# Six edits to a bidirectional gated encoder layer on one core: an 18th pair, sums on VectorE, loads and small steps reordered

## The chip, the core and the metric

The kernel runs on one core of a Trainium2 chip. The metric is device microseconds of one execution, as the median of several runs. The engines are TensorE (PE, with PEld for its weight loads), VectorE (DVE), ScalarE (ACT), GpSimd (POOL) and SyncE (SP, which here only issues DMAs). Times in the text are microseconds (us) unless marked ns.

## The reference, cut to what matters

One layer over x of 1024 positions and 1024 channels, in float32:

```
h  = RMSNorm(x)
glu_in, q, v, z_f, z_b, og, g_a, g_b = split(h @ W_in)        # 1024 + 7*1024 columns
a  = silu(LayerNorm(dwconv31(glu(glu_in)))) @ pw_w            # 512 channels -> 1024
f  = lb + (1 - lb) * sigmoid(z);  key = (1 - lb) * sigmoid(-z) # lb from a softmax of two logits
o  = scan_fwd(silu(q), key_f, v, log f_f) + scan_bwd(...)     # 8 heads of 128, gated linear recurrence
b  = (headnorm(o) * silu(og)) @ o_w
x  = x + (sigmoid(g_a) * a + sigmoid(g_b) * b) @ w_out
h2 = RMSNorm(x)
x  = x + (silu(dwconv3(h2 @ W_gate)) * (h2 @ W_up)) @ w_down  # 2816 hidden
y  = RMSNorm(x)
```

## The kernel before, in words

All activations are kept transposed, channels on partitions and 512 positions ("half" 0 or 1) in a page of 128x512. For precision each fp32 operand is split into a high and a low part, so that every product of 128x128 by 128x512 is three matmuls, in `mm3` (L144 to L146): high by high, high by low, low by high. A split is a cast on ACT (L122) and a subtraction on DVE (L119).

Work is handed out as *jobs*. A job has a `prep` (load of its weights and their split) and a `run`, a generator that gives back control after every piece of 6 matmuls. `run_jobs` runs jobs in order and prepares one job ahead; with `lead` 4 it does so after the first four pieces of the job that runs. `Stream.fill(n)` runs n pieces; this is how matmuls are put between the steps of other work. The order on TensorE is the order in which the program emits it; on the other engines and their DMA queues a planner orders the instructions.

Two kinds of jobs matter here:

- `std_job`: 128 output columns, both halves, 8 blocks of rows: 16 pieces, 96 matmuls.
- `pair_job`: two such column blocks together by Strassen's scheme in the form of seven products of half size, 14 pieces, 84 matmuls. The seven products run in the order 1, 2, 6, 7, 5, 4, 3 (`run`). Their weights are combinations of the four quarters: products 1 and 2 use the rows as loaded; 7 and 5 use `col`, to which a DMA with accumulation added the other column block; 6 and 3 use the rows after two more accumulating DMAs, issued by POOL (L242: `wr<-sw`, `wr<-wr`), which overwrite the rows and so come after the first split has read them. Weight pages "wp" are a ring of four.

The stages, with their times in the profile of before:

1. 0 to 77: load x (`load_x`, four tiles of SP loads), transposes of x for the residual (`residual`, which writes d_x0), first norm of half 0 (`first_norm`), the GLU's first jobs between. `load_vectors` loads a group of small vectors as rows, `turn_vectors` transposes them on TensorE and copies them (L349). v_n holds the first norm's weights.
2. To 471: the rest of the GLU, then the combinations for the pairs (`h_combos`, pages in the ring "su" of four), the lower bounds `lbw` (L691 on), and the stream `s_pairs` of the `NPAIRS` pairs of input columns; between its pieces DVE does the 31 taps of the convolution (`conv_steps`, L755), and then come the LayerNorm and the start of the pointwise jobs. In the LayerNorm of each half, `total` adds the four channel pages into one, and a matmul with ones (L424 for the sum of squares) adds over partitions.
3. To 518.9: the pointwise jobs (8 for each half, two pieces each, operands `ch` in the pool gp0). They are put into the jobs' queue at its front as each half's operands are done:

```
        for i in range(ND):
            job = std_job(
...
            pw_jobs.append(job)
            jobs.insert(at + i, job)
    s_pairs.drain()
```

4. To 975: the scan. Pools p1 and gp0 are released and `hp` takes their place. What input columns the pairs left over (`rest = todo[2 * NPAIRS :]`) become standard jobs of the stream `dense`, with which the scan's steps are interleaved:

```
    cur = Base(scan_inputs(0))
    ins = scan_inputs(1)
    dense.fill(21)
```

`scan_inputs` loads q (L858) and z (L861) of a head and half and makes f and the keys; `scan_base` makes products over blocks of eight positions on DVE (L840, L843: DE, qF, kG); `scan_levels` then doubles the block, each level with a copy on ACT (L945) and matmuls (L948), and between the levels `dense.fill(1.3)`. The pieces left over run at the end of the scan.
5. To 1158: output projection of the scan, merge with the gates, `w_out`, x2 and the FFN's operands.
6. To 1600.8: 22 pairs `ffn_job` (gate and value columns of a block of 128 hidden channels). The second norm's factor `rstd2` is made by two matmuls with ones (L424, then L416) while the first pieces of `s_ffn` run. The evacuation `evac(0, half, ...)` of a gate multiplies by `rstd2` (L1282); after half 1 come the three taps (ACT L1288, DVE L1292, in pages c of the ring "tm" of four), silu, the second factor (L1301), the product with the value (L1302) and the store to d_g.
7. To the end: the down projection in five groups of 4, 4, 5, 5 and 4 blocks of hidden channels; `load_g` loads the g pages of a group (pages of the ring "ev" of three) and splits them; `first_evac` (L1364) copies the first group's sums to `xr`, which later groups add to; the last group adds x2 and makes the last norm.

Of the kernel before, what the change touches and what calls it, by code (L numbers as in the profile page):

```python
# [14 lines left out]
AF = mybir.ActivationFunctionType  # L15
ALU = mybir.AluOpType
# [2 lines left out]
P = 128  # L19
FILL = 1.3  # L20
CONV_FILL = 1.6
NPAIRS = 17
LN_FILL = 6
LN_LAST = 14
GLU_FIRST = 4
# [4 lines left out]
H = 512  # L30
# [15 lines left out]
def tile_hybrid_encoder(  # L46
# [24 lines left out]
    V, A, G, T = nc.vector, nc.scalar, nc.gpsimd, nc.tensor  # L71
# [9 lines left out]
    NH = D // DK  # L81
# [10 lines left out]
    def nm(s):  # L92
        uid[0] += 1
        return f"{s}_{uid[0]}"
# [3 lines left out]
    def bank(tag):  # L98
        return ps.tile([P, H], F32, tag=tag, name=nm(tag), bufs=BANKS[tag])

    def page(pool, tag, bufs, dt=F32):
        return pool.tile([P, H], dt, tag=tag, name=nm(tag), bufs=bufs)
# [4 lines left out]
    def ev():  # L107
        return page(mp, "ev", 3)

    def hx():  # L110
        return page(mp, "hx", 32, F32R)
# [209 lines left out]
    def load_x(half):  # L321
        for i in range(half * 4, half * 4 + 4):
            xt = p0.tile([P, D], F32, tag="xt", name=nm("xt"), bufs=S // P)
            nc.sync.dma_start(xt, x[0, i * P : (i + 1) * P, :])
            x_in.append(xt)

    load_x(0)

    vec_off = {}
    rows_in = []  # L330

    def load_vectors(name, parts):
        n = sum(k for _, _, k in parts)
        r = mp.tile([P, P], F32, tag="tm", name=nm("vr"), bufs=4)
        o = 0
        for key, ap, k in parts:
            nc.sync.dma_start(r[o : o + k, :], ap)
            vec_off[key] = (name, o)
            o += k
        v = cp.tile([P, n], F32, name=name)  # L340
        rows_in.append((v, r, n))
        return v

    def turn_vectors(tag="ob"):
        b = bank(tag)
        for i, (v, r, n) in enumerate(rows_in):
            T.transpose(b[:, i * P : i * P + n], r[:n, :], ident[:n, :n])
        for i, (v, r, n) in enumerate(rows_in):
            V.tensor_copy(v, b[:, i * P : i * P + n])  # L349
        rows_in.clear()  # L350

    def rview(ap):
        r = ap[0]
        if len(r.shape) == 2:
            r = r.rearrange("a b -> (a b)")
        return r.rearrange("(r c) -> r c", c=P)

    vecs = {"v_n": load_vectors("v_n", [("attn", rview(attn_norm_w), ND)])}
    others = {
        "v_a": [  # L360
            ("ffn", rview(ffn_norm_w), ND),
# [71 lines left out]
    def first_norm():  # L433


        xs = x_in[:4]
        ss = cp.tile([P, 4], F32, name=nm("ss"), tag="ss", bufs=2)
        rs = cp.tile([P, 4], F32, name=nm("rs4"), tag="rs4", bufs=1)
        xn = []
        for i, xt in enumerate(xs):  # L440
            t = p0.tile([P, D], F32, tag="xn", name=nm("xn"), bufs=4)
            A.activation(t, xt, AF.Square, accum_out=ss[:, i : i + 1])
            rstd_small(rs[:, i : i + 1], ss[:, i : i + 1], D)
            V.tensor_scalar(t, xt, rs[:, i : i + 1], None, op0=ALU.mult)
            xn.append(t)

        def residual(i, g, tag):
            b = bank(tag)
            for k in range(4):
                T.transpose(  # L450
                    b[:, k * P : (k + 1) * P], xs[i][:, (4 * g + k) * P : (4 * g + k + 1) * P], ident
                )
            t = page(p0, "xr", 7)
            V.tensor_copy(t, b)
            nc.sync.dma_start(
                d_x0[:, i, 4 * g : 4 * g + 4, :], t.rearrange("p (k t) -> p k t", k=4)
            )

        def turn(b, i, k):
            T.transpose(b[:, i * P : (i + 1) * P], xn[i][:, k * P : (k + 1) * P], ident)  # L460

        residual(0, 0, "mm")
        residual(0, 1, "mm")
        turn_vectors("mm")
        banks = [bank(t) for t in ("sc", "tr", "sc", "tr", "ob")]
        for i in range(4):
            for k, b in enumerate(banks):
                turn(b, i, k)
        yield
        late = {2: (1, 0, "mm"), 3: (1, 1, "tr"), 4: (2, 0, "ob")}  # L470
        late |= {5: (2, 1, "sc"), 6: (3, 0, "tr"), 7: (3, 1, "sc")}
        for k in range(ND):
            b, g = banks[k], vec("attn", k)
            hi, lo, raw = hx(), hx(), page(p0, "raw", ND)
            A.activation(hi, b, AF.Copy, scale=g)
            V.scalar_tensor_tensor(lo, b, g, hi.bitcast(F32), op0=ALU.mult, op1=ALU.subtract)  # L476
            A.activation(raw, b, AF.Copy, scale=g)
            nc.sync.dma_start(d_h[k][0], raw)
            ht[1 if k < NK2 else 2].append((hi, lo))
            yield  # L480
            if k + 5 < ND:
                b = bank(("sc", "tr", "sc")[k])
                for i in range(4):
                    turn(b, i, k + 5)
                banks.append(b)
            if k in late:
                residual(*late[k])
# [43 lines left out]
    for j in range(NCW):  # L531
        g = gp0.tile([P, PAD + S + PAD], F32, tag="gl", name=nm("gl"), bufs=NCW)
# [144 lines left out]
    p1 = tc.alloc_tile_pool(name="p1", bufs=1, reuse_waits="tile")  # L677
# [13 lines left out]

    lbl = vecs["v_a"][:, vec_off["lb"][1] : vec_off["lb"][1] + 2 * NH]
    lbw = cp.tile([P, 4, 2 * NH], F32, name="lbw")
    V.tensor_tensor(lbw[:, 0, :], lbl, lbl, op=ALU.max)
    V.tensor_tensor(lbw[:, 0, :], lbl, lbw[:, 0, :], op=ALU.subtract)
    A.activation(lbw[:, 1, :], lbw[:, 0, :], AF.Exp)
    V.reciprocal(lbw[:, 2, :], lbw[:, 1, :])
    V.tensor_tensor(lbw[:, 1, :], lbw[:, 1, :], lbw[:, 2, :], op=ALU.mult)
    V.tensor_tensor(lbw[:, 2, :], lbw[:, 1, :], lbw[:, 1, :], op=ALU.subtract)
# [39 lines left out]

    jobs = collections.deque(in_pair(n) for n in range(1, NPAIRS))  # L740
    jobs.appendleft((lambda: w_pair0, pair0[1]))
# [22 lines left out]


    def total(ts, o):
        G.tensor_tensor(o, ts[0], ts[1], op=ALU.add)
        for t in ts[2:]:
            G.tensor_tensor(o, o, t, op=ALU.add)
        return o  # L770

    pw_jobs = []
# [42 lines left out]

    rest = todo[2 * NPAIRS :]
    rest_jobs = [std_job(in_cols(c), ND, h_std, e) for c, e in rest[:-2]]
# [4 lines left out]
    for k in range(NK2):  # L822
        t = load(d_h[k][1])
        h12.append(split(hx(), hx(), t, V))
    dense = Stream(run_jobs(rest_jobs))
# [297 lines left out]
    NI = 2 * NH  # L1123
    cur = Base(scan_inputs(0))
    ins = scan_inputs(1)
    dense.fill(21)
    pending = Stream(iter(()))
    for h in range(NH):
        Tt = hp.tile([P, 2, 2, 4], F32, tag="Tt", name=nm("Tt"), bufs=3)
# [139 lines left out]
    def ffn_job(j):  # L1269
        g = gp[j % 2]  # L1270
        val = [None, None]

        def evac(e, half, x0, x1=None, op=None):
            if e == 1:
                val[half] = page(fu, "ft", 4)
                V.tensor_tensor(val[half], x0, x1, op=op)
                return
            gh = g[:, 1 + half * H : 1 + (half + 1) * H]
            if x1 is not None:
                V.tensor_tensor(gh, x0, x1, op=op)  # L1280
                x0 = gh
            V.tensor_tensor(gh, x0, rstd2[half], op=ALU.mult)  # L1282
            if half == 0:
                return
            for hf in range(2):
                o = hf * H
                c = tmp()
                A.activation(  # L1288
                    c, g[:, o : o + H], AF.Identity, scale=vec("fdw", j), bias=vec("fdb", j)
                )  # L1290
                for k in (1, 2):
                    V.scalar_tensor_tensor(  # L1292
                        c,
                        g[:, o + k : o + k + H],
                        vec("fdw", k * NF + j),
                        c,
                        op0=ALU.mult,
                        op1=ALU.add,
                    )
                A.activation(c, c, AF.Silu)  # L1300
                V.tensor_tensor(c, c, rstd2[hf], op=ALU.mult)  # L1301
                V.tensor_tensor(val[hf], val[hf], c, op=ALU.mult)  # L1302
                nc.sync.dma_start(d_g[j][hf], val[hf])

        return pair_job(
            w_cols(ffn_w_up, 0, ND, j * P),
            w_cols(ffn_w_up, 0, ND, DFF + j * P),
            NK2,
            lambda i: h2[i],
            fw,  # L1310
            fu,
            evac,
            su=3,
        )

    s_ffn = Stream(run_jobs([ffn_job(j) for j in range(NF)], 4))
    s_ffn.fill(2)
    stats = [rstd_over_partitions(sq, D, "sc", sq) for sq in sq_sum]
    for st in stats:
        next(st)  # L1320
    s_ffn.fill(2)
    rstd2 = [next(st) for st in stats]

    def late_parts(i, src):
# [24 lines left out]
        return hx() if next(n_g) == 0 else page(fd, "gx", 16, F32R)  # L1349

    groups = [4, 4, 5, 5, 4]
    gs, jobs = [], []

    def load_g(f0, n):
        for f in range(f0, f0 + n):
            gs.append([])
            for half in range(2):
                t = ev()
                nc.sync.dma_start(t, d_g[f][half])
                gs[-1].append(split(g_page(), g_page(), t, V))  # L1360

# [132 lines left out]
```

## Time and profile before

| what | us |
|---|---|
| median of 3 runs | 1859.93 (1857.55 to 1863.16) |
| profiled execution | 1873.26 |
| span of the profile (first to last instruction) | 1871.5 |
| PE busy | 1788.6 (96%) |
| DVE busy | 1275.7 (68%) |
| ACT busy | 796.2 (43%) |
| POOL busy | 185.8 (10%) |
| mean granted clock of TensorE | 0.984 |

The profiled execution was 0.7% longer than the median of the runs. The busy time of PE counts a matmul until its modelled end, and matmuls overlap; so the time of a stretch of matmuls is read from its length and the number of matmuls in it. The view of windows gives both, with the granted clock of the stretch. Waits of an engine are read from the view of waits (engine, tile and line that waited, what released it; then the sum in us, how often, the longest) or from the brackets at the end of a row of the timeline.

### The profile page before, as it was taken

How to read it: one execution, taken by the hardware profiler on the slowest of the kernel's cores; microseconds unless marked ns; L12 is line 12 of the kernel's file. 1: busy time of each engine (PE TensorE's matmuls, PEld its weight loads, DVE VectorE, ACT ScalarE, POOL GpSimd, SP SyncE). 2: the span in 40 equal slices, each digit the busy share in tenths (PEclk: the TensorE clock that was granted, in tenths of full speed). 3: DMA queues.
4: the chain of work that ended last, by engine and by line, in shares of the span. 5: the costliest groups of instructions: out<-in, count | busy, mean ns of one | idle time of the engine just before them, and what ended most of it. 6: DMA issues, size and time to landing. Idle time of an engine off the chain costs nothing.

```text
span 1871.5 us, 23768 instructions
## 1 busy us (share of the span) xinstructions
PE 1788.6 (96%) x8574; PEld 1481.4 (79%) x8574; DVE 1275.7 (68%) x1874; ACT 796.2 (43%) x1483; POOL 185.8 (10%) x197
## 2 busy tenths in 40 slices
PE   7989999999999999999989999899999999899996
PEld 6868777777778888888878787688888888788885
DVE  4599999534479999999835565666666667534445
ACT  6443333234545566556442244443444434522124
POOL 1201111213000000000000001111111111000000
PEclk9999999999999999999999999999999999999998
DMA  7658878775653333332238665676776765633134
GB/s 268 213 141 185 184 170 198 184 170 130 208 186 96 113 113 117 98 108 91 74 110 239 191 193 190 152 156 144 150 153 149 156 146 130 208 97 95 55 86 169
DMA packets 323468, 281.42 MB, mean 150 GB/s; under 512 B 14734, under 2 KB 246934, under 8 KB 323350
## 3 DMA queue, kind: packets, MB, share of 16 engines
q1 hardware_dynamic: 272886, 240.05, 41.4%
q0 software_dynamic: 50464, 39.85, 14.9%
q8 instruction: 67, 1.10, 0.3%
q14 instruction: 51, 0.42, 0.1%
HBM read 188.09 MB, written 71.83 MB: 139 GB/s over the span
## 4 chain that ended last, share of the span: by engine, by line
PE 45%; DVE 23%; DMA 18%; ACT 6%; issue 5%; POOL 1%; SPq 0%; ACTq 0%; POOLq 0%; DVEq 0%
PE mm L144 12%; PE mm L145 12%; PE mm L146 12%; DMA wr<-wr 4%; DVE wp L119 3%; DMA wr<-sw 3%; DMA sw<-in_w_in_dram 3%; DMA tm<-d_a 3%; DVE kG L840 2%; DVE acc L755 2%; PE sc L144 2%; PE sc L146 2%; PE sc L145 2%; DVE qF L840 2%; DVE DE L840 2%
## 5 line engine op out<-in xcount | busy, mean ns | idle before, releaser
L144 PE MATMUL mm<-hx,wp 128*128 128x512 f32 x1176 | 480.1, 408 | 23.8 <-DVE ev L541 6.8
L146 PE MATMUL mm<-hx,wp 128*128 128x512 f32 x1176 | 464.9, 395 | 1.9 <-DVE wp L119 1.9
L145 PE MATMUL mm<-hx,wp 128*128 128x512 f32 x1176 | 464.6, 395 | 0.5 <-DVE hx L476 0.5
L122 ACT CAST wp<-wr 128x1024 fp32r<-128x1024 f32 (+2 forms) x193 | 176.7, 915 | 344.8 <-PE mm L145 188.3
L119 DVE TENSOR_TENSOR wp<-wr,wp 128x1024 fp32r<-128x1024 f32 (+2 forms) x193 | 203.4, 1054 | 123.0 <-ACT wp L122 116.2
L144 PEld LDWEIGHTS mm<-hx,wp 128*128 128x128 f32 x1176 | 224.7, 191 | 72.9 <-DVE ev L541 9.7
L146 PEld LDWEIGHTS mm<-hx,wp 128*128 128x128 f32 x1176 | 224.1, 191 | 52.5 <-DVE wp L119 3.7
L145 PEld LDWEIGHTS mm<-hx,wp 128*128 128x128 f32 x1176 | 224.7, 191 | 43.0 <-DVE hx L476 0.8
L755 DVE SCALAR_TENSOR_TENSOR acc<-gl,v_b,acc 128x1024 f32<-128x1024 f32 x120 | 150.0, 1284 | 0.5
L1370 DVE TENSOR_TENSOR xr<-mm,xr 128x512 f32<-128x512 f32 x48 | 33.1, 690 | 80.4 <-PE mm L146 80.4
L948 PE MATMUL sc<-qF,A 128*128 128x128 f32 x512 | 69.8, 280 | 13.3 <-DVE qF L840 13.1
L948 PEld LDWEIGHTS sc<-qF,A 128*128 128x128 f32 x512 | 65.2, 195 | 20.4 <-issue 14.9
L242 POOL DMA_DIRECT2D wr<-sw x38 | 33.8, 889 | 442.8 <-DVE wp L119 153.1
L122 ACT CAST wq<-sw 128x1024 fp32r<-128x1024 f32 x39 | 41.0, 1051 | 77.1 <-PE mm L145 59.5
L945 ACT COPY A<-kG 128x512 f32<-128x512 f32 x64 | 39.6, 618 | 73.8 <-DVE kG L840 51.3
L1292 DVE SCALAR_TENSOR_TENSOR tm<-gp,v_a,tm 128x512 f32<-128x512 f32 x88 | 65.6, 746 | 3.3 <-ACT tm L1288 2.5
L144 PE MATMUL mm<-hy,wp 128*128 128x512 f32 x156 | 62.2, 399 | 3.1 <-ACT su L270 2.9
L145 PE MATMUL mm<-hy,wp 128*128 128x512 f32 x156 | 61.9, 396 | 0.7 <-DVE hy L119 0.7
L270 ACT COPY su<-mm 128x512 f32<-128x512 f32 x78 | 45.1, 578 | 39.2 <-PE mm L146 39.2
L144 PE MATMUL tr<-hx,wp 128*128 128x512 f32 x156 | 61.4, 394 | 0.0
L146 PE MATMUL mm<-hy,wp 128*128 128x512 f32 x156 | 61.1, 392 | 0.0
L144 PE MATMUL sc<-hy,wq 128*128 128x512 f32 x156 | 61.1, 392 | 0.0
(322 smaller groups left out, 3601.5 us busy)
## 6 DMA issues: line engine op xcount, KB each, us to landing
wr<-in_w_in_dram SPq DMA_DIRECT2D x53, 512.0 KB
sw<-in_ffn_w_up_dram SPq DMA_DIRECT2D x44, 256.0 KB
sw<-in_ffn_w_up_dram POOLq DMA_DIRECT2D x22, 512.0 KB, 9.2
wr<-in_ffn_w_up_dram SPq DMA_DIRECT2D x22, 512.0 KB
d_g<-ft SPq DMA_DIRECT2D x44, 256.0 KB
ev<-d_g SPq DMA_DIRECT2D x44, 256.0 KB
wr<-sw POOLq DMA_DIRECT2D x38, 256.0 KB, 3.2
wr<-wr POOLq DMA_DIRECT2D x38, 256.0 KB, 4.8
```

Source lines behind the costliest of these rows:

```text
L119: eng.tensor_tensor(lo, src, hi.bitcast(F32), op=ALU.subtract)
L122: A.copy(hi, src)
L144: T.matmul(acc, whi[:, k, :], ahi, start=first, stop=False, skip_group_check=again)
L145: T.matmul(acc, whi[:, k, :], alo, start=False, stop=False, skip_group_check=again)
L146: T.matmul(acc, wlo[:, k, :], ahi, start=False, stop=last, skip_group_check=again)
L242: G.dma_start(o, a, accum_op=ALU.add)
L270: A.copy(t, acc)
L755: V.scalar_tensor_tensor(acc, g[:, k : k + S], tap(k), acc, op0=ALU.mult, op1=ALU.add)
L840: V.tensor_tensor(o, a, b, op=op)
L945: A.copy(A_t.rearrange("p (b x e) -> p b x e", x=2, e=h), pairs(kG, h))
L948: T.matmul(b[:, c * P : (c + 1) * P].rearrange("p (b x e) -> p b x e", x=2, e=h), A_t[:, c * P : (c + 1) * P], view(qF, c * P, [[2 * h, P ...
L1292: V.scalar_tensor_tensor(c, g[:, o + k : o + k + H], vec("fdw", k * NF + j), c, op0=ALU.mult, op1=ALU.add,)
```

## The change

Six edits:

- The first norm's weights are loaded ahead of x, and their transposes run ahead of the two residual ones.
- The lower bounds' first two steps work in a page of the ring "su" instead of the constant tile `lbw`, so that they wait for their turn in that ring.
- `total` adds on VectorE instead of GpSimd.
- There are 18 pairs instead of 17, so that two column blocks fewer are left for `dense`, and `dense.fill(21)` ahead of the scan is `dense.fill(5)`.
- The FFN multiplies half 0 of the gate by `rstd2` only when half 1 comes, and 5 pieces instead of 2 run between the two matmuls of the second norm's sums.
- The g loads take their pages from the rings "ev" and "tm" in a cycle of seven.

```diff
-NPAIRS = 17
+NPAIRS = 18
...
-    load_x(0)
-
     vec_off = {}
...
     vecs = {"v_n": load_vectors("v_n", [("attn", rview(attn_norm_w), ND)])}
+    load_x(0)
...
+        turn_vectors("mm")
         residual(0, 0, "mm")
         residual(0, 1, "mm")
-        turn_vectors("mm")
         banks = [bank(t) for t in ("sc", "tr", "sc", "tr", "ob")]
...
     lbw = cp.tile([P, 4, 2 * NH], F32, name="lbw")
-    V.tensor_tensor(lbw[:, 0, :], lbl, lbl, op=ALU.max)
-    V.tensor_tensor(lbw[:, 0, :], lbl, lbw[:, 0, :], op=ALU.subtract)
-    A.activation(lbw[:, 1, :], lbw[:, 0, :], AF.Exp)
+    lbt = page(p1, "su", 4)[:, : 2 * NH]
+    V.tensor_tensor(lbt, lbl, lbl, op=ALU.max)
+    V.tensor_tensor(lbt, lbl, lbt, op=ALU.subtract)
+    A.activation(lbw[:, 1, :], lbt, AF.Exp)
...
     def total(ts, o):
-        G.tensor_tensor(o, ts[0], ts[1], op=ALU.add)
+        V.tensor_tensor(o, ts[0], ts[1], op=ALU.add)
         for t in ts[2:]:
-            G.tensor_tensor(o, o, t, op=ALU.add)
+            V.tensor_tensor(o, o, t, op=ALU.add)
         return o
...
-    dense.fill(21)
+    dense.fill(5)
...
             gh = g[:, 1 + half * H : 1 + (half + 1) * H]
-            if x1 is not None:
+            if half == 0:
                 V.tensor_tensor(gh, x0, x1, op=op)
-                x0 = gh
-            V.tensor_tensor(gh, x0, rstd2[half], op=ALU.mult)
-            if half == 0:
                 return
+            V.tensor_tensor(g[:, 1 : 1 + H], g[:, 1 : 1 + H], rstd2[0], op=ALU.mult)
+            V.tensor_tensor(gh, x0, rstd2[1], op=ALU.mult)
             for hf in range(2):
...
-    s_ffn.fill(2)
+    s_ffn.fill(5)
     rstd2 = [next(st) for st in stats]
...
-    gs, jobs = [], []
+    gs = []
+    n_in = itertools.cycle([ev, tmp, ev, tmp, ev, tmp, tmp])
...
-                t = ev()
+                t = next(n_in)()
                 nc.sync.dma_start(t, d_g[f][half])
```

## The prediction

> **What bounds the kernel now.** I read the page first (sections 1 and 2), then the work of each stage in windows, then the waits and the timelines around the places that the change touches.
>
> ```profile
> span 1871.5 us, 23768 instructions
> PE 1788.6 (96%) x8574; PEld 1481.4 (79%) x8574; DVE 1275.7 (68%) x1874; ACT 796.2 (43%) x1483; POOL 185.8 (10%) x197
> DVE  4599999534479999999835565666666667534445
> ```
> ```profile
> 0.00:77.00 77.00, 67.59 (x320) 55.51 (x321) 32.70 (x43) 43.73 (x69) 16.98 (x34) 0.98 0.76 255
> 77.00:340.00 263.00, 251.23 (x1081) 203.88 (x1080) 250.48 (x275) 101.81 (x143) 38.44 (x36) 0.99 0.74 174
> 494.60:518.90 24.30, 24.06 (x103) 18.85 (x103) 9.17 (x13) 11.84 (x21) 0.63 (x2) 1.00 0.69 212
> 518.90:547.40 28.50, 28.50 (x127) 23.61 (x126) 18.88 (x29) 18.65 (x29) 0.53 (x1) 1.00 0.73 226
> 547.40:975.00 427.60, 402.58 (x2538) 353.65 (x2537) 372.72 (x691) 226.51 (x528) 15.62 (x16) 0.99 0.31 99
> 1202.00:1600.80 398.80, 397.96 (x1730) 324.12 (x1729) 263.67 (x352) 165.14 (x232) 64.36 (x59) 1.00 0.69 149
> ```
>
> In a window row the second number is its length, then busy time of PE, weight loads, DVE, ACT, POOL, then the granted clock. TensorE is the bound nearly everywhere: 96% of the span, 397.96 of 398.80 us in the FFN. DVE is full as well in two stages, the first pairs with the convolution's taps (250.48 of 263) and the scan (372.72 of 427.60, nines and eights in its slices). So removed matmuls pay where PE is alone, and a wait of PE costs unless other matmuls stand in front of it. From 518.9 to 547.4, 126 products of 128x512 run without a gap: 28.50/126 = 0.226 us each, the price of one below.
>
> **Part 1, the 18th pair and the fill of 21 that becomes 5.** A pair takes 84 products where two plain jobs took 96. Pairs and the pointwise jobs share one queue, in which pair 17 comes to stand between the two pointwise halves: the jobs of the first half were put in ahead of it, those of the second half behind it, since the queue has not reached it by then. What follows the second half is the scan, and it starts like this:
>
> ```profile
> 518.61 0.40 PE L146 MATMUL mm<-ch,wp 128*128 128x512 f32 x1
> 519.04 0.46 SPq L858 DMA_DIRECT2D q<-d_q  x1
>   POOL DE L834: 42.6, 1
> 521.67 0.92 SPq L861 DMA_DIRECT2D zi<-d_z  x2
> 525.69 0.63 ACT L862 ACTIVATE k<-zi 128x512 f32<-128x512 f32 x1 [3.11 <-DMA zi<-d_z]
> 535.03 1.22 DVE L119 TENSOR_TENSOR wp<-wr,wp 128x1024 fp32r<-128x1024 f32 x1
> 542.34 1.22 DVE L840 TENSOR_TENSOR kG<-Kh,DE 128x1024 f32<-128x1024 f32 x1
> 545.55 0.61 ACT L945 COPY A<-kG 128x512 f32<-128x512 f32 x1
> 547.43 1.05 PE L948 MATMUL sc<-qF,A 128*128 128x128 f32 x8
> ```
>
> The first row is the last pointwise matmul. The scan's pages lie where the pointwise operands lay: POOL's first memset of DE waited 42.6 us for these matmuls, and the scan's q load goes out 0.4 us after the last of them starts. Then a chain runs: z loads, sigmoids, the base on DVE, a copy, and the first matmul of the scan at 547.43, 28.6 us after the last pointwise product (its successor started at 518.85). In the kernel before, the 21 dense pieces of 6 products (126 x 0.226 = 28.5 us) fill exactly this stretch. After the change 5 pieces, 6.8 us, are left. The chain doesn't shorten with them, but for weight splits like that at 535.03, of which two lie in it and fall away or move: 2 x 1.22 = 2.4, and I take 26.0 us in place of 28.6. PE then idles 26.0 - 6.8 = 19.2 us. The pieces inside the scan are 145 and those behind it 10 in both kernels, and the scan is set by DVE, so nothing gives it back.
>
> Against the kernel before, the scan starts later by the pair, 84 x 0.226 = 19.0, and earlier by the 2.6 of the chain. It also starts earlier by what the second pointwise half lost at its start, since the pair now covers that: 24.30 us for 103 products is 24.30 - 103 x 0.226 = 1.0. Pair 17 has a wait of its own:
>
> ```profile
> wr<-sw POOLq DMA_DIRECT2D x38, 256.0 KB, 3.2
> wr<-wr POOLq DMA_DIRECT2D x38, 256.0 KB, 4.8
> 519.74 1.05 ACT L122 CAST wp<-wr 128x1024 fp32r<-128x1024 f32 x1 [2.06 <-DMA wr<-in_w_in_dram]
> PE mm L144 <- ACT su L270: 4.3, 1, 4.3
> ```
>
> A pair's third product needs weights that two accumulating DMAs make, and these can start only once the rows are split. Behind another pair they have a whole pair's time. Behind short pointwise jobs the split waits for weight pages that the last job but one holds, and ends about when the pair starts (estimate: 12 products = 2.7 us ahead, less 1.05 cast and 1.22 subtraction and some latency). Then 3.2 + 4.8, two issues of about 0.5 and a cast of 1.05 make 10 us; the product is due after 24 x 0.226 = 5.4. So PE waits 4 to 5 us. The nearest row is the same wait in the FFN, whose second pair follows a first one that could not prepare ahead (job 1's third product): 4.3 us. With the slow clock behind it (part 2) I take 6.0, between 0 and 10.
> Sum of part 1: 19.0 + 6.0 - 1.0 - 2.6 = **+21.4** (+11 if the chain is 7 us shorter and the wait is nearly gone; +25 if the wait is 10).
>
> **Part 2, the channel sums on VectorE.**
>
> ```profile
> 424.02 2.95 POOL L769 TENSOR_TENSOR tm<-tm,tm 128x512 f32<-128x512 f32 x2
> 427.02 1.56 PE L424 MATMUL ob<-ones_m,tm 128*128 128x1 f32 x8 [2.06 <-POOL tm L769]
> DVE r L428 <- PE ob L424: 4.1, 1, 4.1
> 428.45:433.70 5.25, 5.25 (x13) 4.11 (x14) 1.39 (x2) 1.28 (x4) 2.59 (x3) 0.50 0.80 130
> 1608.21 0.69 DVE L1302 TENSOR_TENSOR ft<-ft,tm 128x512 f32<-128x512 f32 x1
> ```
>
> POOL adds two pages in about 1.5 us, DVE multiplies two in 0.69. The last sum of squares came late and PE waited 2.06 us for it; DVE stood idle then (it waited 4.1 for PE's answer). Three adds at 0.69 instead of 4.55 on POOL end some 2.5 us earlier, so that wait goes. Behind it PE ran at a granted clock of 0.50: products at 0.43 us instead of 0.226 (12 of them lie between 428.45 and 433.70, so about 12 x 0.2 = 2.5, and 0.3 for the small ones). With the wait the slow stretch goes: 2.06 + 2.8 = **-4.9**. Twelve adds cost DVE 8.3 us in a stage where it is half idle: nothing.
> The Trainium skill ("TensorE: Matmul & The Clock Gate", "What's actually happening") lets the clock fall after an idle window of about 3.4 us. Here it fell behind 2.06 us, so the row doesn't bear that out as a threshold; by the page, the slow stretch has another cause and stays. That is rival D.
>
> **Part 3, the first norm's weights ahead of x.**
>
> ```profile
> 2.58 0.40 SPq L337 DMA_DIRECT2D vr<-in_attn_norm_w_dram  x1
> 14.84 0.69 ACT L475 ACTIVATE hx<-sc,v_n 128x512 fp32r<-128x512 f32 x1 [1.47 <-DVE v_n L349]
> ```
>
> ACT waited 1.47 us for v_n, whose copy stood on DVE behind two residual copies. That wait goes; each x load goes out 0.44 later: about -1.2 + 0.4, **-0.7** (-1.5 to +0.5).
>
> **Part 4, lower bounds later.** Six small DVE operations leave the place where the Exp stood, but stay in the saturated stage of 77 to 340, so DVE has the same sum.
>
> ```profile
> 99.50 1.28 ACT L591 ACT_TABLE_LOAD   x1
> PE mm L144 <- ACT tm L591: 2.9, 1, 2.9
> ```
>
> The Exp costs a table load of 1.28 and the return to the sigmoids this one, and PE waited 2.9 there. That may go, but with DVE as the bound of the stage it isn't on the path; and the page from the "su" ring can delay a pair's copy by a slot. **0** (-1.3 to +2).
>
> **Part 5, the second norm's scale later, with five pieces ahead instead of two.**
>
> ```profile
> PE sc L416 <- ACT tm L415: 3.1, 2, 1.8
> ```
>
> Three more pieces cover these 3.1 us of waiting. But the next stop is job 1's third product, the wait of 4.3 above, whose weights come by a chain of DMAs that doesn't start earlier; PE reaches it sooner and waits longer. **-0.5** (-3 to +2). The scale of half 0 moves to where DVE idles.
>
> **Part 6, g loads in two rings.**
>
> ```profile
> 1604.30 0.43 SPq L115 DMA_DIRECT2D tm<-d_x  x1
> 1610.62 0.68 DVE L1302 TENSOR_TENSOR ft<-ft,tm 128x512 f32<-128x512 f32 x1
> 1609.53 4.10 DMA ev<-d_g
> PE mm L144 <- ACT xr L1364: 5.7, 1, 5.7
> 1611.80:1618.60 6.80, 3.79 (x9) 3.02 (x10) 2.69 (x5) 3.29 (x6) 0.00 (x0) 0.50 0.94 299
> ```
>
> Before, PE did the first 36 products of the down projection by 1608.9 (from 1600.8), then waited 5.7 for a copy that stood on ACT behind the casts of g, and lost 1.8 more at the slow clock: its effective time for the 36 is 1600.8 + 15.9. The tm ring has four slots, used in turn, and the FFN's last two conv pages hold two of them: they are read for the last time at 1608.21 and 1610.62. The four tm pages of group 0 are g 0 half 1, 1 half 1, 2 half 1 and 3 half 0; the fourth comes into the slot read at 1610.62. (The loads of d_x, which use this ring now, go out from 1604.30 on although their data is old, which fits that.) But 3 half 0 is wanted by the very first job, as its fourth k: PE does 9 products and stops until 1611.3 + 4.1 (a g load) + about 0.7 for the cast = 1616.1, 15.3 to 15.7 after the FFN's end. The other 27 products take 6.1: 1600.8 + 22. That is **+6.3** (+4.8 to +8).
>
> **Sum:** 21.4 - 4.9 - 0.7 + 0 - 0.5 + 6.3 = +21.6. The profiled execution took 1873.26, 0.7% above the median of 1859.93, so I add the difference to the median: 1859.93 + 21.6 = **1881.5**. All low ends together give +4, all high ends +36.
>
> **Rivals.**
> A, the scan's inputs go out before the last pointwise matmul. If at least 19 us earlier, pair 17 and the second half cover the chain, PE's 19.2 us of idling go, and the sum is +2.4: 1862, no slower than can be told. For it: q and z were stored hundreds of us before. Against it: the wait of 42.6 and the q load 0.4 us behind that matmul. It decides from the moment at which q is loaded before the second half ends. 0.08.
> B, g loads aren't held by the tm ring. Then two rings feed ACT earlier, and the wait of 5.7 with its 1.8 goes: -7.5 in place of +6.3, sum +7.8, 1867.7. Against it stand the two L1302 rows. 0.13.
> C, pair 17's third product is in time (its rows are split sooner than I think): 6.0 less, 1875.5. 0.15.
> D, the slow clock behind the sums stays: +2.8, 1884.3. 0.1.
>
> **How the numbers follow.** The forecast has 0.54. From 1866 (B with a shorter chain) to 1892 (the wait in pair 17 at 10, part 6 at +8, part 5 at +2) all but A and some tails lie inside. About 0.3%, 5.6 us, is what a measurement of this kernel can tell: A alone is within it, A with B or C is faster, the lowest ends of B are within it. Faster 0.04, same 0.08, slower 0.88.
>
> **What would show it.** Right: PE idle some 19 us between the fifth dense piece and the first scan level; a wait of 4 us in pair 17 behind its second product; no L424 wait for the sums; a stop after 9 products of the down projection until g 3 half 0 has landed. Wrong: a q load well ahead of the last pointwise matmul; f3's g load before 1610.62's counterpart; pair 17 elsewhere than between the pointwise halves.

## The result, and the profile after

The changed kernel took 1885.15 us (median of 5 runs, 1877.18 to 1891.92), the kernel before 1861.05 (5 runs, 1857.55 to 1864.15): ratio 1.0127, 95% interval 1.0093 to 1.0161. That is 24 us slower (17 to 30); the forecast was 21.6 slower. The profiled execution of after took 1877.18 us, the shortest of its five. That of before took 1873.26, longer than every other run of its kernel on record (at most 1868.80), at a mean granted clock of 0.984 where the runs beside the experiments had 0.986 to 0.993. So the two spans differ by 3.9 us alone, and a stage of before is taken as typical only where the profiles of the experiments agree with it.

Page of the kernel after, sections 1 and 2:

```profile
span 1875.4 us, 23729 instructions
PE 1780.0 (95%) x8562; PEld 1474.8 (79%) x8562; DVE 1281.0 (68%) x1891; ACT 798.6 (43%) x1484; POOL 173.3 (9%) x188
PE   8989999999969999999989999899999999899996
```

There are 12 matmuls fewer, as a pair (84) for two plain jobs (96) makes them. (So a plain job over 8 blocks of rows, both halves, has 8 pieces and 48 matmuls; 16 and 96 are those of two.) In the row of PE a 6 has come in among the nines at the twelfth slice, 516 to 562 us. By stages, first windows of before (pointwise jobs; the scan from its first level to its last; the down projection), then of after (pointwise jobs with pair 17; the stretch ahead of the scan; the scan; the down projection), with the columns as in the prediction:

```profile
471.10:518.90 47.80, 47.56 (x204) 36.87 (x203) 20.82 (x33) 26.12 (x49) 1.86 (x4) 1.00 0.69 218
547.40:944.40 397.00, 376.13 (x2396) 331.54 (x2395) 365.35 (x676) 213.79 (x490) 13.79 (x14) 0.99 0.32 101
1600.80:1871.50 270.70, 250.36 (x1121) 205.56 (x1119) 125.08 (x193) 82.83 (x233) 2.43 (x4) 0.97 0.38 115
```
```profile
462.10:533.70 71.60, 67.81 (x288) 53.76 (x287) 26.01 (x39) 30.73 (x55) 3.65 (x6) 0.98 0.57 177
540.20:558.20 18.00, 0.34 (x2) 0.00 (x0) 14.13 (x25) 11.87 (x20) 0.00 (x0) 0.60 0.54 167
558.20:951.80 393.60, 375.58 (x2396) 331.81 (x2397) 365.49 (x677) 213.56 (x490) 13.83 (x14) 0.99 0.31 100
1600.70:1875.40 274.70, 254.73 (x1121) 207.43 (x1119) 130.03 (x200) 87.34 (x241) 2.42 (x4) 0.96 0.37 118
```

From the first pointwise product to the first level of the scan it was 76.3 us (471.1 to 547.4) and is 96.1 (462.1 to 558.2): 19.8 more. In after, TensorE stands still for nearly 18 us of this stretch. The profiles of the experiments bear the 19.8 out: the stretch is 75 to 77 us with 16 or 17 pairs and 96 to 98 with 18. The scan has the same 2396 matmuls and is 3.4 shorter, but the experiments with 17 pairs show 394 to 397 us for it, so that is no effect of the change. The down projection is 4.0 longer.

The start of the scan in the timelines of after (PE, SP, ACT), which answers to the nine rows of before:

```profile
533.31 0.40 PE L146 MATMUL mm<-ch,wp 128*128 128x512 f32 x1
533.74 0.51 SPq L858 DMA_DIRECT2D q<-d_q  x1
535.87 0.91 SPq L861 DMA_DIRECT2D zi<-d_z  x2
540.15 0.39 PE L146 MATMUL mm<-hx,wp 128*128 128x512 f32 x1
557.59 0.60 ACT L945 COPY A<-kG 128x512 f32<-128x512 f32 x1
558.24 1.01 PE L948 MATMUL sc<-qF,A 128*128 128x128 f32 x3 [17.70 <-ACT A L945]
```

The last pointwise matmul still releases the q load, 0.4 us later; the five dense pieces end at 540.5, and TensorE waits 17.70 us for the chain of loads, sigmoids, base and copy. From the end of the last pointwise product (533.55) to the first level it is 24.7 us. In before this stretch was 28.6 us, but there the copy ended at 545.55 + 0.61 = 546.16 and TensorE, still at the dense pieces, took up the level at 547.43 without a wait. So the chain itself took 27.3 us in before and 24.6 in after.

### The profile page after: what moved, and what is told of

It is laid out like the page before. It is cut to its first block, busy times and chain, and to the rows that moved or that the text cites. A ratio compares the mean times of both kernels' runs of the same rounds, so it can differ in the third digit from the quotient of the medians.

```text
span 1875.4 us, 23729 instructions
## 1 busy us (share of the span) xinstructions
PE 1780.0 (95%) x8562; PEld 1474.8 (79%) x8562; DVE 1281.0 (68%) x1891; ACT 798.6 (43%) x1484; POOL 173.3 (9%) x188
## 4 chain that ended last, share of the span: by engine, by line
PE 59%; DVE 20%; DMA 11%; ACT 5%; issue 4%; POOL 1%; SPq 0%; DVEq 0%; ACTq 0%; POOLq 0%
PE mm L144 14%; PE mm L145 14%; PE mm L146 14%; PE sc L146 3%; PE sc L144 3%; PE sc L145 3%; DVE acc L755 2%; DMA tm<-d_a 2%; DVE wp L119 2%; DMA sw<-in_w_in_dram 2%; DVE kG L840 2%; DMA wr<-wr 1%; PE tr L144 1%; PE tr L145 1%; PE tr L146 1%
## 5 line engine op out<-in xcount | busy, mean ns | idle before, releaser
L144 PE MATMUL mm<-hx,wp 128*128 128x512 f32 x1152 | 467.4, 406 | 16.0 <-DVE ev L540 6.5
L146 PE MATMUL mm<-hx,wp 128*128 128x512 f32 x1152 | 452.7, 393 | 2.8 <-DVE wp L119 2.8
L145 PE MATMUL mm<-hx,wp 128*128 128x512 f32 x1152 | 452.8, 393 | 2.0 <-DVE hx L475 1.4
L144 PEld LDWEIGHTS mm<-hx,wp 128*128 128x128 f32 x1152 | 218.3, 189 | 62.3 <-DVE ev L540 9.2
L146 PEld LDWEIGHTS mm<-hx,wp 128*128 128x128 f32 x1152 | 217.9, 189 | 52.4 <-DVE wp L119 5.0
L145 PEld LDWEIGHTS mm<-hx,wp 128*128 128x128 f32 x1152 | 218.3, 189 | 44.4 <-DVE hx L119 2.3
L948 PE MATMUL sc<-qF,A 128*128 128x128 f32 x512 | 69.4, 279 | 27.8 <-ACT A L945 17.7
L144 PE MATMUL mm<-hy,wp 128*128 128x512 f32 x160 | 64.7, 404 | 10.1 <-DVE ft L1276 4.6
L1276 DVE TENSOR_TENSOR ft<-su,mm 128x512 f32<-128x512 f32 x22 | 15.1, 688 | 76.3 <-issue 69.6
L270 ACT COPY su<-mm 128x512 f32<-128x512 f32 x80 | 46.5, 581 | 44.0 <-PE mm L146 42.9
L145 PE MATMUL mm<-hy,wp 128*128 128x512 f32 x160 | 64.2, 401 | 0.0
L146 PE MATMUL mm<-hy,wp 128*128 128x512 f32 x160 | 63.6, 398 | 0.3 <-DVE wp L119 0.3
```

The lines of the kernel that those rows point to most:

```text
L144: T.matmul(acc, whi[:, k, :], ahi, start=first, stop=False, skip_group_check=again)
L145: T.matmul(acc, whi[:, k, :], alo, start=False, stop=False, skip_group_check=again)
L146: T.matmul(acc, wlo[:, k, :], ahi, start=False, stop=last, skip_group_check=again)
L270: A.copy(t, acc)
L948: T.matmul(b[:, c * P : (c + 1) * P].rearrange("p (b x e) -> p b x e", x=2, e=h), A_t[:, c * P : (c + 1) * P], view(qF, c * P, [[2 * h, P ...
```

## The experiments

Each kernel ran against the kernel before on the same chip; ratios are this over before, with 95% intervals. "Slower" and "faster" in us are the ratio times the median of before in the same comparison.

**1. The pair and the fill alone**, in the kernel before.

```diff
-NPAIRS = 17
+NPAIRS = 18
...
-    dense.fill(21)
+    dense.fill(5)
```

> Only the 18th pair and the fill of 5 are taken over. The theory of the prediction: pair 17 stands between the pointwise halves, and the 14 pieces lost ahead of the scan leave TensorE idle some 18 to 19 us before the first scan level; 17 to 22 us slower than before. Rival: the pair pays for itself and the loss of the whole change comes from the other edits; then within 6 us of before.

1878.81 us, ratio 1.0099 (1.0070 to 1.0128): 18.4 us slower. Timeline of TensorE in this run:

```profile
561.02 1.22 PE L948 MATMUL sc<-qF,A 128*128 128x128 f32 x4 [17.84 <-ACT A L945]
```

The idle stretch is there with this one edit, and it brings most of the loss.

**2. The change without the pair**, the other five edits kept; against the changed kernel:

```diff
-NPAIRS = 18
+NPAIRS = 17
...
-    dense.fill(5)
+    dense.fill(21)
```

> The changed kernel with 17 pairs and the fill of 21 again; the other five edits stay. The sum of the prediction for those gives +0.2 us against before; if the wait for the sums only moved to the next matmul with ones, about +4. Rival (the other edits carry the loss): +15 to +24.

1863.42 us, ratio 1.0019 (1.0002 to 1.0037): 3.5 slower. The five edits together neither carry the loss nor give the gain that part 2 promised. The loss of the two rings (experiment 8) is among them, so the other four gain some 3 us (an estimate from two runs that are each uncertain by 3).

**3. The channel sums alone**, in the kernel before.

```diff
-        G.tensor_tensor(o, ts[0], ts[1], op=ALU.add)
+        V.tensor_tensor(o, ts[0], ts[1], op=ALU.add)
         for t in ts[2:]:
-            G.tensor_tensor(o, o, t, op=ALU.add)
+            V.tensor_tensor(o, o, t, op=ALU.add)
```

> Only the channel sums on VectorE. The prediction: the wait of 2.06 us and the slow clock behind it go, 4.9 us faster. Rival, from the changed kernel's trace: TensorE reaches the next matmul with ones (rstd) sooner and waits there about 2.3 us for the chain on POOL and ACT, with the slow clock behind it; 0 to 2 us faster.

1859.04 us, ratio 0.9996 (0.9977 to 1.0014): no difference. Timeline of TensorE and windows, first of the kernel after, then of this one:

```profile
417.00 0.94 PE L423 MATMUL ob<-ones_m,tm 128*128 128x1 f32 x8
424.49 2.07 PE L415 MATMUL ob<-tm,ones_m 128*128 128x512 f32 x2 [2.30 <-ACT tm L414]
424.50:427.90 3.40, 3.40 (x7) 2.03 (x8) 0.68 (x2) 0.59 (x1) 0.00 (x0) 0.54 1.05 130
```
```profile
421.30 0.95 PE L424 MATMUL ob<-ones_m,tm 128*128 128x1 f32 x8
428.70 1.23 PE L416 MATMUL ob<-tm,ones_m 128*128 128x512 f32 x2 [2.21 <-ACT tm L415]
428.70:432.10 3.40, 3.40 (x8) 2.38 (x9) 1.51 (x3) 0.59 (x1) 0.00 (x0) 0.63 0.85 106
```

The first matmul with ones no longer waits. The second (L415 in after, L416 in before) comes three pieces behind it, and the chain between them, over DVE, POOL and ACT, is longer than three pieces: a wait of 2.2 to 2.3 us takes the place of the one of 2.06, and in these two traces the slow clock comes behind it as it did in before.

**4. The change with all g loads in "ev"**; against the changed kernel:

```diff
-    n_in = itertools.cycle([ev, tmp, ev, tmp, ev, tmp, tmp])
+    n_in = itertools.cycle([ev])
```

> The changed kernel with all g loads in the ring ev again. The prediction put the two rings at a loss of 6.3 us, so this is 6 us faster than the changed kernel, about 15 us slower than before; the changed kernel's trace makes the loss about 4, so 17 to 20 slower than before. Rival B (two rings help): 7 us slower than the changed kernel, about 31 slower than before.

1878.48 us, ratio 1.0093 (1.0065 to 1.0121): 17.3 slower than before. The whole change has 1.0127, so some 6 to 7 us come from the two rings, though the two intervals overlap; experiment 8 has it by itself.

**5. The 18th pair with the idle stretch filled**, in the kernel before.

```diff
-FILL = 1.3
+FILL = 1.2
...
-NPAIRS = 17
+NPAIRS = 18
...
-    dense.fill(21)
+    dense.fill(17)
```

> As the kernel with the 18th pair alone, but with 17 pieces ahead of the scan and 1.2 in place of 1.3 between its steps, so that some 11 of the pieces inside the scan move into the idle stretch ahead of it. The prediction's claim that VectorE sets the scan: the idle stretch is filled, but the scan starts at the same point and is no shorter; 15 to 22 us slower than before, as with the pair alone. Rival (TensorE sets the scan): the scan is 11 x 1.36 = 15 us shorter, and the kernel is 0 to 5 us slower than before.

1874.99 us, ratio 1.0104 (1.0083 to 1.0124): 19.3 slower. Windows of this kernel, the stretch ahead of the scan and the scan:

```profile
539.60:565.80 26.20, 23.25 (x103) 18.89 (x101) 17.70 (x28) 17.75 (x28) 0.53 (x1) 1.00 0.71 236
565.80:955.00 389.20, 364.06 (x2330) 319.71 (x2331) 362.94 (x675) 211.56 (x486) 15.23 (x14) 0.99 0.30 99
```

TensorE is busy for 23.25 of the 26.20 us now, and nothing is gained. The scan has 66 products fewer, 15 us of TensorE, but is only 4.4 shorter than after's, while DVE's time in it is the same (362.94 against 365.49). What looked like 18 us of waste was the visible part of a chain that takes its 25 to 27 us whether TensorE is filled or not.

**6. 16 pairs, more pieces in the scan**, in the kernel before.

```diff
-FILL = 1.3
+FILL = 1.45
...
-NPAIRS = 17
+NPAIRS = 16
```

> The other way: 16 pairs, 21 pieces ahead of the scan, and 1.45 in place of 1.3 between its steps, so that the 16 pieces of the two further plain jobs run inside the scan. If the scan is set by VectorE and its gaps on TensorE (some 25 us in the kernel before) take 16 x 1.36 = 21.8 us of pieces, the 84 products of the pair, 19 us, are saved: 12 to 19 us faster than before. Rival: with that much more work TensorE sets the scan; within 6 us of before.

1874.06 us, ratio 1.0093 (1.0072 to 1.0115): 17.3 slower, outside what both theories gave. The scan in windows, and two rows of TensorE's timeline:

```profile
535.60:952.90 417.30, 397.91 (x2492) 350.50 (x2492) 371.78 (x678) 218.68 (x497) 16.27 (x14) 0.99 0.31 101
```
```profile
454.47 1.86 PE L424 MATMUL ob<-ones_m,tm 128*128 128x1 f32 x8 [6.09 <-POOL tm L769]
459.27 1.22 PE L416 MATMUL ob<-tm,ones_m 128*128 128x512 f32 x1 [2.94 <-ACT tm L415]
```

The scan takes 96 products more and is 20.3 longer than in before: they pay about their full price of 96 x 0.226 = 21.7. VectorE's own time grows by 6.4 us only (371.78 against 365.35), too little to account for it, and the gaps on TensorE (21 us in before) were not filled. We read the gaps as waits inside the scan's own chain, which hold no further pieces; no run takes that chain apart. And the pair that is gone was the cover of the second half's LayerNorm: waits of 6.1 and 2.9 us appear there. So of the numbers tried the kernel before stands at a balance: fewer pieces in the scan save little, more cost all.

**7. The FFN's edits alone**, in the kernel before: half 0's scale as in the change, and

```diff
-    s_ffn.fill(2)
+    s_ffn.fill(5)
     rstd2 = [next(st) for st in stats]
```

> Only the second norm's scale later with five pieces. The prediction: 0.5 us faster, since job 1's third product waits longer for its weights by what is gained. Rival, from the changed kernel's trace, where the FFN was some 4 us shorter: 4 us faster.

1857.02 us, ratio 1.0005 (0.9987 to 1.0023): no difference. The waits of TensorE at the start of the FFN, of after and of this kernel:

```profile
PE mm L144 <- DVE ft L1276: 4.6, 1, 4.6
PE sc L415 <- ACT rs L416: 0.8, 1, 0.8
```
```profile
PE mm L144 <- DVE ft L1276: 4.5, 1, 4.5
PE sc L416 <- ACT rs L417: 0.8, 1, 0.8
```

The waits of 3.1 at L416 are down to 0.8, the one of 4.3 at job 1's third product is gone, and a wait of 4.5 stands at the last product of job 0 (product 3). It adds to a bank that DVE has to read first (L1276), and that reading stands on DVE behind splits of weights and operands. The wait moved, as in experiment 3.

**8. g loads in turn, half 0 from "ev", half 1 from "tm"**, in the kernel before.

```diff
-    gs, jobs = [], []
+    gs = []
+    n_in = itertools.cycle([ev, tmp])
...
-                t = ev()
+                t = next(n_in)()
```

> The kernel before with g loads in two rings in turn: half 0 of each from ev, half 1 from tm, so that no page of the first job lies in a tm slot of the last conv pages. If the loss of the two rings comes from a page of the first job that waits for such a slot: it is gone, 2 to 7 us faster than before. If it comes from ACT's order (casts of g that stand behind the last pair's silu): it stays, about 5 us slower than before.

1864.65 us, ratio 1.0038 (1.0021 to 1.0054): 7.1 slower, the second of the two theories. ACT's timeline at the end of the FFN, of after and of this kernel, each with TensorE's wait there:

```profile
1600.72 0.62 ACT L122 CAST wp<-wr 128x512 fp32r<-128x512 f32 x1 [7.54 <-PE mm L145]
1601.63 0.81 ACT L1287 ACTIVATE tm<-gp,v_c,v_a 128x512 f32<-128x512 f32 x1 [0.29 <-DVE gp L1283]
1603.43 0.60 ACT L122 CAST hx<-tm 128x512 fp32r<-128x512 f32 x1
1605.48 0.60 ACT L122 CAST hx<-ev 128x512 fp32r<-128x512 f32 x1
PE mm L144 <- ACT hx L122: 4.6, 1, 4.6
```
```profile
1597.64 0.62 ACT L122 CAST wp<-wr 128x512 fp32r<-128x512 f32 x1 [7.54 <-PE mm L145]
1602.39 0.60 ACT L122 CAST hx<-ev 128x512 fp32r<-128x512 f32 x1
PE mm L144 <- ACT hx L122: 4.6, 1, 4.6
```

ACT runs its instructions in the order in which the planner put them. With two rings the planner puts the cast of a down projection's weights ahead of the casts of g; its page comes free only with the last pair's products, and ACT stands for 7.54 us, while casts of g pages whose loads had gone out by 1592 (in after) stand behind it. Then come the last pair's taps and silu, and only then the casts that the first down job's second k needs.

**9. The sums on VectorE with five pieces between the matmuls with ones**: experiment 3 and, in the LayerNorm,

```diff
         next(rstd)
-        s_pairs.fill(3)
+        s_pairs.fill(5)
         rs = next(rstd)
```

> The channel sums on VectorE, and five pieces of pairs instead of three between the two matmuls with ones of each half (L424, L416), so that the wait that took the place of the one removed is covered too. The prediction's price for wait and slow clock, 4.9 us, then comes: 4 to 5 us faster than before, with no wait of TensorE at either matmul and no stretch at a clock of 0.50 behind them. Rival: something else is next (the weights of the pair that runs there), and it stays within 2 us of before.

1856.63 us, ratio 0.9978 (0.9961 to 0.9996): 4.1 faster. Windows behind L424, which starts at 425.98:

```profile
425.90:429.30 3.40, 3.40 (x21) 2.91 (x20) 1.39 (x2) 1.53 (x2) 0.78 (x2) 1.00 0.79 252
429.30:432.70 3.40, 3.23 (x15) 2.34 (x13) 0.00 (x0) 1.27 (x4) 2.09 (x2) 1.00 0.69 155
```

Neither matmul waits, and the clock stays at 1.00.

**10. Two rings from the second group on**: experiment 8 with

```diff
-                t = next(n_in)()
+                t = ev() if f < groups[0] else next(n_in)()
```

> The kernel before with g loads in two rings only from the second group on; the first group stays in ev. If the loss of the two rings comes from ACT's order at the start of the down projection (a weight cast that waits for the last pair stands ahead of the casts of g), that order is the old one here: within 2 us of before. Rival: the loss comes from the later groups; 5 to 9 us slower than before.

1860.75 us, ratio 0.9997 (0.9978 to 1.0015): no difference. The cast of the weights on ACT, the waits of TensorE at the start of the down projection and the projection as a window, of this kernel; then the window of experiment 8:

```profile
1596.10 0.62 ACT L122 CAST wp<-wr 128x512 fp32r<-128x512 f32 x1 [1.41 <-PE mm L145]
PE mm L144 <- ACT xr L1365: 1.9, 1, 1.9
1596.40:1862.90 266.50, 249.87 (x1120) 205.12 (x1118) 124.72 (x192) 82.62 (x233) 2.43 (x4) 0.97 0.37 117
```
```profile
1597.60:1870.30 272.70, 252.86 (x1121) 206.28 (x1119) 130.32 (x200) 87.16 (x241) 2.43 (x4) 0.96 0.37 119
```

With group 0 as it was, the weights' cast comes behind six casts of g and holds ACT for 1.41 us, not 7.54. The stop behind the casts is gone, and 6.2 us of the window with it; that the later groups use two rings costs nothing that can be told. The other profiles agree: the projection takes 266 to 271 us in the ten whose first group is in "ev" alone, and 273 to 275 in the three with two rings (after, experiments 2 and 8).

**11. The small edits together**: the change without the pair and its fill and without the two rings, and with the five pieces of experiment 9; against the changed kernel:

```diff
-NPAIRS = 18
+NPAIRS = 17
...
-        s_pairs.fill(3)
+        s_pairs.fill(5)
...
-    dense.fill(5)
+    dense.fill(21)
...
-                t = next(n_in)()
+                t = ev()
```

> All edits but the pair and the two rings, with the five pieces between the matmuls with ones: first norm's weights ahead, lower bounds later, sums on VectorE, the FFN's scale later. The prediction's terms add up to 4.9 + 0.7 + 0 + 0.5 = 6.1 us faster than before. From the runs so far (sums -0.7, FFN +1.2, each about 3 us uncertain) 0 to 5 us faster.

1854.80 us, ratio 0.9963 (0.9947 to 0.9979): 6.9 faster than before (3.9 to 9.9). This is the version that beats both. How much of it is experiment 9's edit (4.1 by itself, 0.7 to 7.3) and how much the others' can't be told from these intervals.

## Why the prediction was right, point by point

**Part 1** (+21.4 forecast): +18.4 measured alone (13 to 24), +19.8 from the first pointwise product to the scan in the traces. Its terms: pair 17 took 25.2 us (486.08 to 511.27) for the 19.0 of its products, so it lost 6.2, where 6.0 was taken for its late third product. Two rows of after, from its first product and its third:

```profile
487.30 0.50 PE L146 MATMUL mm<-hx,wp 128*128 128x512 f32 x1 [0.53 <-DVE wp L119]
495.55 0.53 PE L144 MATMUL mm<-hy,wp 128*128 128x512 f32 x1 [2.96 <-ACT wp L122]
```

The wait of the third product is 3 us long, not 4 to 5; the twelve products behind it, at a clock that falls to 0.50, lose 2 more. The remaining 0.9 is lost in the pair's first product, which waited for the split of its own weights, a term that the sum did not have. The chain was over-estimated: 24.7, not 26.0, so TensorE idles 17.7 and not 19.2. The 28.6 that the estimate started from was the length of the dense pieces; the copy's own row had the chain's end 1.3 us earlier. Rivals A and C fell: the q load went out 0.4 us after the last pointwise matmul had started, and the third product was late. The claim that VectorE sets the scan fits the run with fewer pieces (experiment 5) and not the one with more (experiment 6).

**Part 2** (-4.9): -0.7 (-4.3 to +2.6). The step that failed is "with the wait the slow stretch goes": it asked how early the sums would be ready, not what TensorE would wait for next. The price fits: with the next wait covered as well, 4.1 came (0.7 to 7.3, experiment 9). On rival D, the Trainium skill's idle window of about 3.4 us ("TensorE: Matmul & The Clock Gate", "What's actually happening"): waits of 2.06, 2.21 and 2.30 us were each followed by a clock of 0.50 to 0.63, and in experiment 9 there was neither. So in this kernel waits shorter than that window can be enough. They need not be. In experiment 2, whose code up to this place is that of after, the same wait stands and the clock behind it stays full:

```profile
428.63 1.12 PE L415 MATMUL ob<-tm,ones_m 128*128 128x512 f32 x2 [2.08 <-ACT tm L414]
428.60:432.00 3.40, 3.37 (x13) 2.47 (x14) 1.59 (x3) 1.64 (x2) 0.00 (x0) 1.00 0.85 107
```

In experiment 4 it is the same (a wait of 2.42 us, a clock of 1.00 behind it). So the 2.8 us of slow clock are not always part of the price, and what decides on them stays open.

**Part 3** (-0.7): in after, TensorE turns the weights at 2.45 and ACT's first scaled copy starts earlier:

```profile
2.45 0.24 PE L345 MATMUL mm<-ident,vr 8*128 8x8 f32 x1 [2.45 <-DMA vr<-in_attn_norm_w_dram]
13.15 0.68 ACT L474 ACTIVATE hx<-sc,v_n 128x512 fp32r<-128x512 f32 x1
```

It was at 14.84: 1.7 earlier, just past the good end of the range. It was not run by itself. Its forecast is below what these runs can tell.

**Part 4** (0): the Exp's table load is at 124.04 now, and the wait at the sigmoid of the GLU is half as long:

```profile
124.04 1.28 ACT L696 ACT_TABLE_LOAD   x1
PE mm L144 <- ACT tm L590: 1.4, 1, 1.4
```

It was 2.9 before; a wait of 1.4 for a copy on ACT (L270) stands in the same stretch of after, where before had 0.4. Whether this reaches the end of the stage was not tried. In the profiles, the four kernels with the edits of parts 2 to 4 come to the first pointwise product after 462.1 to 465.7 us and the two with part 2 alone after 466.2 and 467.5, which may be a gain of parts 3 and 4; but kernels with the same code differ there by up to 6 us.

**Part 5** (-0.5): +0.9 (-2.4 to +4.3). That the gain would be waited away was right; the place was not. The wait stands at job 0's last product and for DVE's queue, not at job 1's third product. Nor did the old wait of 4.3 there end on a DMA, as the prediction took it. Its row names a copy on ACT (L270), and in before's ACT timeline that copy stands behind a cast of weights whose own wait ended with the pair's second product:

```profile
1192.38 1.04 ACT L122 CAST wp<-wr 128x1024 fp32r<-128x1024 f32 x1 [7.49 <-PE tr L146]
1195.99 0.57 ACT L270 COPY su<-mm 128x512 f32<-128x512 f32 x1
```

So it was no fair model for pair 17 in part 1 either, whose weights did come late by DMA: their cast waited 3.96 us for the second accumulation.

**Part 6** (+6.3): 7.1 in experiment 8 (3.9 to 10.0), 6.2 in the windows of 8 and 10. The mechanism was wrong, that the size came out was luck, and rival B fell. TensorE stopped after 3 products of the down projection, not after 9, and not for a page of the ring but for ACT's order. The fourth page of "tm" did not wait for the conv page read last either: in after's SP timeline two g loads go out at 1605.96, behind the first conv page's last reading and the first g split; the slot read at 1607.23 served a later load. The row that says what stood ahead on ACT could not be seen in the trace of before, where the casts of g came first. On the luck: the first 36 products were to take 22 us and take 18.3 in after, and the 15.9 of before that they were set against held a wait of 5.7 us for a copy on ACT, which is 1.9 to 3.9 in every other kernel with the first group in "ev". Both ends of the difference were some 4 us too long.

**The sum** (+21.6 forecast, 24 measured, 17 to 30) stands on part 1, whose mechanism the runs show and whose size was right within what they can tell (+18.4 by itself, some 20 in the traces). Part 2 was wrong by some 4 us, part 6 right by luck, and parts 3 and 4 were not measured; that the rest adds up so well is chance. The ends of the parts' ranges add to about +5 and +33, not to +4 and +36 (with rival D the upper end is +35).

## What to carry to other kernels

Where filler work covers a dependency chain, count the chain from the event that releases it (here the last reader of the memory that its inputs take) before you move the filler: work put ahead of that event covers nothing of it. If the filler runs up to the chain's end, take the chain's length from its last link and not from the next instruction on TensorE. A wait that is removed is worth its price only if the next wait of the same engine is covered too; experiments 3 and 9 are the same edit without and with that, and in experiment 7 the wait moved too. Where an engine takes its instructions in a fixed order, as ACT did here, a new ring for loads can change what stands ahead of their casts; look for an instruction there that waits for something late.

## What the runs showed that was not expected

Waits of TensorE of 2.1 to 2.3 us in before, after and experiment 3 were each followed by a granted clock of 0.50 to 0.63 in the next 3.4 us and more, which cost more than the wait (2.8 us in before by the prediction's count). The same wait in experiments 2 and 4 was not. A price read from one execution can hold such a stretch by chance, and before's profile held more slow clock than the other runs of that kernel. And the scan, with VectorE at 365 of 397 us and TensorE idle for 21, took next to none of 96 further products for free. As we read it, neither engine was the bound by itself but the chain between them; that is argued from two runs, not shown.
